# Expert weights in 8 KB pieces: one expert a load, gate before up before down, in a two-block fp32 kernel

## The chip, the cores and the metric

The kernel runs on one core of one Trainium2 chip. The metric is the device time of one execution in microseconds (us), lower is better. A timed run is one launch of the whole program; the profile is one further execution, recorded by the hardware profiler.

## The reference

Two transformer blocks follow one another on 512 tokens of 1024 channels, all in fp32. The first block mixes tokens in four ways (neighbourhood attention, gated delta net, differential attention, Fourier mixing) and ends in a mixture of experts; the second has latent attention, a gating unit, pooling and a dense feed-forward, twice. The change touches the mixture of experts alone:

```python
def expert_choice_ffn(h, w_router, w_gate, w_up, w_down):
    B, N, D = h.shape                      # 1, 512, 1024
    cap = EC_FACTOR * N // N_EXPERTS       # 64 tokens for each of 16 experts
    aff = jax.nn.softmax((h @ w_router).astype(F32), axis=-1)
    gate, idx = lax.top_k(jnp.swapaxes(aff, 1, 2), cap)
    xg = jax.vmap(lambda hb, ib: hb[ib])(h, idx)
    hid = jax.nn.silu(jnp.einsum('becd,edf->becf', xg, w_gate)) * jnp.einsum('becd,edf->becf', xg, w_up)
    y = jnp.einsum('becf,efd->becd', hid, w_down) * gate[..., None].astype(h.dtype)
    return jax.vmap(lambda yb, ib: jnp.zeros((N, D), yb.dtype).at[ib.reshape(-1)].add(yb.reshape(-1, D)))(y, idx)
```

Each expert has a gate and an up matrix of 1024 x 2048 and a down matrix of 2048 x 1024, 8 MB each, so the sixteen experts' weights are 384 units of 1 MB (402.7 million bytes), each read from HBM once.

## The kernel before

`block1` runs up to the router, `experts` does the mixture, `block2` the second block. `experts` takes the experts in eight pairs. In a pair the 64 tokens of expert A and the 64 of expert B stand side by side as 128 rows: `gather` (L1981) picks them with one-hot products into `xg`; the gate and up products (L2012) go to PSUM tiles `a`, rows 0 to 63 from one expert's weights and rows 64 to 127 from the other's; the hidden rows `hid` are SiLU of gate (ScalarE, L2020) times up (VectorE, L2021); four transposes (L2024) and a copy (L2026) make `hT`; the down products (L2033) gather in `y`; and eight products `o` with the one-hot matrix (L2048, L2049) add the result to the rows it came from (L2050). The pair is done in two halves `fp` of 1024 hidden columns each.

Weights come as *units* of 1 MB, 8 KB in each of 128 partitions. `expert_units` lists them in the order of use: a unit holds, for both experts of the pair, 1024 fp32 (4 KB) of one row per partition. `Stream` issues them all from SyncE's queue at L93, each into the next slot of a ring of slots that lie in several pools: 12 slots are there from the start of the output projection of block 1 (`ahead(12)`), 6 more come free there, and one, `w9`, with the pool of `experts`, 19 in all. A load waits only until its slot's earlier unit has been used. So SyncE's order is fixed by the list, and how far it runs ahead by the number of slots. `block2` then loads its own weights in the same queue (L283).

Of the kernel before, what the change touches and what calls it, by code (L numbers as in the profile page):

```python
# [6 lines left out]
F32 = mybir.dt.float32  # L7
# [33 lines left out]
class Ring:  # L41
    """slots of 8 KB per partition from several pools, taken in turn"""
# [10 lines left out]
class Carve:  # L53
    """arrays next to one another in tiles of 8 KB per partition"""
# [16 lines left out]
class Cut:  # L71
    """arrays next to one another in one tile"""
# [11 lines left out]
class Stream:  # L84
    """units of weights in the order of their use, loaded as far ahead as asked for"""
# [20 lines left out]
def prep2(tc, k, I, cs, ps, two):  # L106
    """everything of block 2 that does not depend on x"""
# [22 lines left out]
    # rope tables  # L130
# [18 lines left out]
def prep3(k, I, cs, ps, tmp):  # L149
    """the rest of it: rows over all partitions, and the matrices of the gating unit and of the pooling"""  # L150
# [34 lines left out]
def split(k, pool, src, shape, tag="", nb=4, eng=None):  # L185
    """(hi, lo) of an fp32 array, as tiles that the one-pass products take"""
    nc = k.nc
    n = shape[0] * shape[1]
    wsz = max(n, k.wsz)
    hi = pool.tile([P, wsz], F32R, tag="wh" + tag, name="wh", bufs=nb)  # L190
    lo = pool.tile([P, wsz], F32R, tag="wl" + tag, name="wl", bufs=nb)
    hv = hi[:, :n].rearrange("p (a b) -> p a b", a=shape[0])
    lv = lo[:, :n].rearrange("p (a b) -> p a b", a=shape[0])
    nc.scalar.activation(hv, src, AF.Copy)  # L194
    (eng or nc.vector).tensor_tensor(lv, src, hv.bitcast(F32), op=OP.subtract)  # L195
    return hv, lv
# [14 lines left out]
class Joint:  # L211
    """the final norm of the first block and the first norm of the second: x * g1 * g2 in two parts, and both sums of squares"""
# [24 lines left out]
    def done(self, ps, sp):  # L237
        """the factor of the final norm, and the inverse square and the factor of both"""
# [15 lines left out]
        # eps and the mean square after the final norm, times its inverse factor squared  # L254
# [15 lines left out]
def block2(tc, k, I, xT, out, ps):  # L270
# [3 lines left out]
    with ExitStack() as ctx:  # L274
# [20 lines left out]
        class Prep:  # L295
            """x * g in two parts, and the sum of squares of x over its channels"""
# [21 lines left out]
            def rstd(self):  # L318
                """mean square + eps, and its -1/2 power, [token, tile]"""
# [10 lines left out]
        def rowcast(pool, r):  # L330
            """[token, tile] -> the same row on all partitions"""
# [9 lines left out]
        def finish():  # L341
            """the final norm of the first block in its place"""
            rb = rowcast(sqp, pr.r0)
            for d in range(8):
                nc.vector.scalar_tensor_tensor(xT[:, d], xT[:, d], k.gf[:, d:d + 1], rb, op0=OP.mult, op1=OP.mult)

        def result(c):
            """half of the channels, token-major"""
# [12 lines left out]
        for l in range(2):  # L361
            win = I['w_in_2'][l].rearrange("(k p) f -> p k f", p=P)
            with tc.tile_pool(name=f"att{l}", bufs=1) as at:
                e1 = None
                # low-rank queries and keys/values, channel-major
# [37 lines left out]
                # token-major: shared rotary key, gates and values of the spatial unit, pool  # L403
                zn = at.tile([P, 4, 800], F32, name="zn")

                def rest(c):
                    """a part of these columns"""
# [19 lines left out]
                # queries, keys, values, token-major  # L427
# [23 lines left out]
                def queries(tb):  # L451
# [13 lines left out]
                    # sums of squares per head  # L465
# [6 lines left out]
                    # rotary part of the queries  # L472
# [12 lines left out]
                def keys(tb):  # L485
                    T2 = slice(2 * tb, 2 * tb + 2)
                    # keys
# [32 lines left out]
                def group(gi, c0, gn):  # L520
                    """the norm of a group of the mix, and its channels in two parts"""
# [17 lines left out]
                def gating():  # L539
                    # spatial gating unit  # L540
# [106 lines left out]
                def outs(h, mix, done, pt_):  # L647
                    """half of the rows of the out projection"""
# [33 lines left out]
                # out projection  # L682
# [3 lines left out]
            # feed-forward  # L686
# [55 lines left out]
def consts1():  # L742
# [40 lines left out]
    # first those that are needed beyond the first block's attention  # L783
# [19 lines left out]
def rev(ap, axis):  # L803
    """the same elements, one axis back to front"""
# [10 lines left out]
def exp_poly(nc, sp, out, x, n):  # L815
    """exp(x), x <= 0, to float32's accuracy"""
# [18 lines left out]
def block1(tc, k, I):  # L835
    """up to the router: x1 (channel-major), its norm token-major, slots and weights of the experts"""
# [16 lines left out]
    with ExitStack() as ctx:  # L853
# [29 lines left out]
        def wcols(c0, n, eng=None):  # L883
            """8 k-tiles of n columns of w_in, split"""
# [15 lines left out]
        def chan(w, c, z, src, n, ds=range(8)):  # L900
            """z[128 channels, n tokens]"""
# [4 lines left out]
        def modulation(cg, pool, unit):  # L906
            """2048 columns of the modulation; one step per unit of weights"""
# [17 lines left out]
        with tc.tile_pool(name="e1", bufs=1) as e1, tc.tile_pool(name="e2", bufs=2) as e2:  # L925
# [21 lines left out]
            # squares  # L947
# [9 lines left out]
            # shift and scale, of the rows and of the context's  # L957
# [5 lines left out]
            # shift and scale of two tiles of channels at a time, for both conditions, and these tiles of the normed rows  # L963
            def first(p):
                """the part of these tiles in the first convolution's channels"""
# [4 lines left out]
            for p in range(4):  # L970
# [6 lines left out]
                # the rows' tiles meanwhile  # L977
# [45 lines left out]
        p1c = ExitStack()  # L1023
        pc = p1c.enter_context(tc.tile_pool(name="pc", bufs=1))
        # places that stay free until the chain, for the weights of the other modulations
# [16 lines left out]
        def halves(out, z4, w, ctx):  # L1042
            """natural tiles -> pairs of an even chunk and the odd chunk that mirrors it"""
# [7 lines left out]
        # places of a convolution's rows that are free until the arrays of the other mixers come  # L1051
# [41 lines left out]
        def l2(kind, X, n, o, XT):  # L1093
            """divided by the norm of each head; channel-major too"""
# [27 lines left out]
        # gates  # L1122
# [38 lines left out]
        # by type of step: A runs the even chunk forward and the odd one backward, B the reverse  # L1161
# [34 lines left out]
        # products of keys within chunks  # L1196
# [23 lines left out]
        # decays  # L1220
# [26 lines left out]
        # the queries with the decay of their place, for both types of step  # L1247
# [35 lines left out]
        for t in range(2):  # L1283
            for q in range(4):
                rows = slice(32 * q, 32 * q + 32)
                fwd = q // 2 == t
                # the system is lower triangular: as it is forward, transposed backward
# [11 lines left out]
        # back: the inverse with its second index on the partitions, and for half of the blocks its first  # L1299
# [36 lines left out]
        cosv, sinv = (C(n).rearrange("p (t i) -> p t i", t=4) for n in ('cos', 'sin'))  # L1336

        def rope(x, n):
            """pairs of neighbours turned by the angles of their token, in place"""
# [27 lines left out]
        # the queries of each head, their first part twice, and their second part  # L1367
# [12 lines left out]
        def before(si):  # L1380
            """the inverse of the step's triangular systems, what it makes of the keys, and of the values"""
# [16 lines left out]
        def state(si, T, wn):  # L1398
            """the step's new values and the next state"""
# [51 lines left out]
        def dn_norm(ps_):  # L1451
            """norm and gate of two pairs of chunks"""
# [52 lines left out]
        for c in range(2):  # L1505
            z = zt("qz")
            chan(w, c, z, lat, 512)
            # each tile of queries back to front, as the bias comes
# [15 lines left out]
        def put(mx, j, z, s=None):  # L1524
            """channels of the mix in two parts"""
# [17 lines left out]
        # the keys of each head in both parts, the first one where the queries' second part is  # L1543
# [59 lines left out]
        def score(*qk):  # L1603
            """queries times keys"""
# [6 lines left out]
        def values(A, v, h, alt=False):  # L1611
            """weights times values [query, 64], by way of [key, query], three blocks of keys at a time"""
# [34 lines left out]

        def df_head(h):
# [41 lines left out]
            # by the root mean square of the head  # L1690
# [52 lines left out]
        # the out projection: the rows that are there before the last heads, then the others  # L1743
# [75 lines left out]
        def logits():  # L1819
            """of the channels up to 6 [token, expert], in the bank that the sums of squares come to as well"""  # L1820
# [62 lines left out]
        # the normed tokens, token-major  # L1883
# [6 lines left out]
        # the first pair's tokens by the number of those that come before each: larger, or as large and earlier  # L1890
# [40 lines left out]
def expert_units(I):  # L1931
    """the weights of a pair of experts after another, a megabyte at a time"""
    w = [I[n][0].rearrange("e (k p) f -> p e k f", p=P) for n in ('w_gate', 'w_up', 'w_down')]
    for e in range(0, 16, 2):
        for fp in range(2):
            for kk in range(8):
                for i in range(2):
                    yield w[i][:, e:e + 2, kk, fp * 1024:fp * 1024 + 1024], 2
            for kk in range(8 * fp, 8 * fp + 8):
                yield w[2][:, e:e + 2, kk], 2  # L1940


def experts(tc, k, I, prep, ps):
    """the tokens that each expert chose, through it, and added to the rows they came from"""
# [3 lines left out]
    def places(xp):  # L1948
        """of the other experts' tokens: the largest eight at a time, counted in the tokens' order"""
# [5 lines left out]
        nc.vector.tensor_copy(wk, z[0:16])  # L1955
        for i in range(8):
# [5 lines left out]
        nc.vector.tensor_tensor(wk, wk, cum, op=OP.mult)  # L1962
        z = ps.tile([P, 512], F32, tag="m", name="slot", bufs=2)
# [4 lines left out]
    with tc.tile_pool(name="x2", bufs=2) as xp:  # L1968
        k.stream.ring.order.append((xp, "w9", 1))
        for pr in range(8):  # L1970
# [16 lines left out]
            def slots():  # L1987
                """the slots in the order [slot, token], and the weight of the token in each"""
# [16 lines left out]
            for fp in range(2):  # L2005
# [131 lines left out]
```

## Time and profile before

| | |
|---|---|
| three timed runs | 2605.61, 2611.21, 2605.61 us (median 2605.61) |
| span of the profiled execution, first to last instruction | 2604.2 us |
| stage of the experts, from the first L2012 to the last L2049 | 579.4 to about 1540 us |
| TensorE's granted clock in that stage from 585 us on | 1.00 |
| rate of all DMAs, 620 to 1500 us | 408 GB/s |

The page gives no time of its own for the profiled execution beside the span; the median of the runs lies 1.4 us above the span, and that is taken for what lies around it. A view by stage gives, for a stretch, each engine's busy time and the rate of DMA; a view of DMA gives packets by size and the share of time that they took on the 16 DMA engines (over 100% where packets overlap); the timeline merges neighbouring instructions of one kind, and in brackets stands the idle time before the first and what ended it. The trace counts two MATMUL records for one fp32 product.

### The profile page before, as it was taken

The page shows a single profiled execution, that of the slowest core. Times are in us where ns is not written, and L with a number is a line of the kernel's source. Part 1 is how long each engine was busy: PE and PEld are TensorE (multiplying, and loading weights), DVE is VectorE, ACT ScalarE, POOL GpSimd, SP SyncE. Part 2 cuts the span into 40 slices and gives each one's busy share as a digit, 9 for nine tenths or more (in the row PEclk, how much of TensorE's full clock was granted, in tenths as well). Part 3 has the DMA queues.
Part 4 walks back from the last instruction along what each step waited for, and adds up shares of the span by engine and source line. Part 5 has one row for each costly group of instructions (what it writes and reads, how often), then busy time and mean ns, then how long its engine had stood idle before and what let it go on. Part 6 is the DMA issues. An engine that isn't in the chain of part 4 may idle for free. (4 is left out here: it accounts for less than half of the span.)

```text
span 2604.2 us, 31722 instructions
## 1 busy us (share of the span) xinstructions
PE 2420.6 (93%) x12919; PEld 1602.7 (62%) x12919; DVE 1040.3 (40%) x1839; ACT 700.7 (27%) x1362; POOL 254.3 (10%) x331
## 2 busy tenths in 40 slices
PE   6988999989999797989898889999999999999999
PEld 5768877763434242323233349778888897788887
DVE  5798347532111011010101036664444556644443
ACT  4522347520000000000000035432222354422221
POOL 1344445300000000000000012000000020000000
PEclk9998999989999999999999999999999999999999
DMA  8441100479999999999999972133332221322220
GB/s 270 149 145 47 48 22 17 150 258 399 407 408 408 409 408 408 409 409 409 409 409 409 409 254 86 49 113 97 98 97 87 65 82 49 113 97 89 91 96 33
DMA packets 214584, 547.75 MB, mean 210 GB/s; under 512 B 19183, under 2 KB 100903, under 8 KB 212263
## 3 DMA queue, kind: packets, MB, share of 16 engines
q1 hardware_dynamic: 208272, 544.39, 55.7%
q10 hardware_dynamic: 6167, 1.33, 0.3%
q8 instruction: 102, 1.67, 0.3%
q14 instruction: 43, 0.35, 0.0%
HBM read 543.56 MB, written 2.13 MB: 210 GB/s over the span
## 5 line engine op out<-in xcount | busy, mean ns | idle before, releaser
L2012 PE MATMUL a<-w,xg 128*64 128x512 f32 x2048 | 477.4, 598 | 59.7 <-DMA w<-in_w_up_dram 31.2
L2012 PEld LDWEIGHTS a<-w,xg 128*64 128x64 f32 x2048 | 139.3, 136 | 369.7 <-issue 236.6
L194 ACT ACTIVATE wh<-w 128x512 fp32r<-128x512 f32 (+3 forms) x304 | 202.6, 678 | 457.4 <-PE gu L201 226.6
L202 PE MATMUL gu<-hh,wl 128*128 128x512 f32 x704 | 278.1, 395 | 0.0
L2033 PE MATMUL y<-w,hT 128*64 128x512 f32 x1024 | 248.6, 599 | 31.1 <-DMA w<-in_w_down_dram 19.3
L201 PE MATMUL gu<-hl,wh 128*128 128x512 f32 x704 | 276.7, 393 | 0.0
L200 PE MATMUL gu<-hh,wh 128*128 128x512 f32 x704 | 273.8, 389 | 0.0
L195 DVE TENSOR_TENSOR wl<-w,wh 128x512 fp32r<-128x512 f32 (+3 forms) x304 | 223.8, 749 | 121.4 <-ACT wh L194 119.5
L2021 DVE TENSOR_TENSOR hid<-a,hid 128x512 f32<-128x512 f32 x32 | 22.1, 692 | 486.0 <-PE a L2012 486.0
L2033 PEld LDWEIGHTS y<-w,hT 128*64 128x64 f32 x1024 | 75.7, 136 | 182.0 <-issue 120.2
L2020 ACT ACTIVATE hid<-a 128x512 f32<-128x512 f32 x32 | 19.1, 597 | 550.8 <-PE a L2012 502.1
L201 PEld LDWEIGHTS gu<-hl,wh 128*128 128x128 f32 x704 | 132.4, 188 | 30.9
L200 PEld LDWEIGHTS gu<-hh,wh 128*128 128x128 f32 x704 | 132.5, 188 | 29.7
L202 PEld LDWEIGHTS gu<-hh,wl 128*128 128x128 f32 x704 | 132.8, 189 | 26.4
L200 PE MATMUL dn<-hid,wh 128*128 128x512 f32 x352 | 139.3, 401 | 0.0
L202 PE MATMUL dn<-hid,wl 128*128 128x512 f32 x352 | 137.7, 395 | 0.0
L201 PE MATMUL dn<-hid,wh 128*128 128x512 f32 x352 | 137.3, 394 | 0.0
L732 DVE TENSOR_TENSOR accT<-dn,accT 128x512 f32<-128x512 f32 x96 | 66.1, 691 | 125.7 <-PE dn L202 125.7
L241 POOL MEMSET gg<- 128x256 f32 x1 | 0.3, 314 | 960.3 <-PE y L2033 960.3
L1985 ACT ACTIVATE xg<-g,mT,sc 128x128 f32<-128x128 f32 x64 | 25.9, 454 | 208.2 <-PE g L1981 208.2
L1999 DVE COPY wt<-wt 64x1 f32<-64x1 f32 x16 | 2.5, 156 | 191.7 <-PE wt L1996 191.6
L201 PEld LDWEIGHTS dn<-hid,wh 128*128 128x128 f32 x352 | 66.1, 188 | 17.8 <-DVE hid L722 2.3
(695 smaller groups left out, 4057.5 us busy)
## 6 DMA issues: line engine op xcount, KB each, us to landing
w<-in_w_gate_dram SPq DMA_DIRECT2D x150, 1024.0 KB, 7.2
w<-in_w_up_dram SPq DMA_DIRECT2D x150, 1024.0 KB, 20.4
w<-in_w_down_dram SPq DMA_DIRECT2D x150, 1024.0 KB, 20.4
w<-in_w_mod_dram SPq DMA_DIRECT2D x24, 1024.0 KB, 9.7
w<-in_w_in_dram SPq DMA_DIRECT2D x16, 1024.0 KB, 5.3
w<-in_w_out_dram SPq DMA_DIRECT2D x8, 1024.0 KB, 4.9
wo<-in_w_out_dram SPq DMA_DIRECT2D x4, 1024.0 KB, 9.9
w<-in_w_in_dram SPq DMA_DIRECT2D x4, 576.0 KB, 3.8
```

Source lines behind the costliest of these rows:

```text
L194: nc.scalar.activation(hv, src, AF.Copy)
L195: (eng or nc.vector).tensor_tensor(lv, src, hv.bitcast(F32), op=OP.subtract)
L200: nc.tensor.matmul(out, a[0], b[0], start=start, stop=False)
L201: nc.tensor.matmul(out, a[0], b[1], start=False, stop=False)
L202: nc.tensor.matmul(out, a[1], b[0], start=False, stop=stop)
L732: nc.vector.tensor_tensor(xT[:, d], z, xT[:, d], op=OP.add)
L1985: nc.scalar.activation(xg[:, dd, :], g[:, d, :], AF.Identity, scale=k.sc2[:, dd:dd + 1], bias=k.mT[:, 0, 24 + dd:25 + dd])
L1999: nc.vector.tensor_copy(wt[64 * i:64 * i + 64], tp[64 * i:64 * i + 64, 0, i:i + 1])
L2012: nc.tensor.matmul(a[f][64 * i:64 * i + 64, :], xg[:, kk, 64 * i:64 * i + 64], u[:, i, f * 512:f * 512 + 512], start=kk == 0, stop=kk == 7)
L2020: nc.scalar.activation(hid, acc[0][f], AF.Silu)
L2021: nc.vector.tensor_tensor(hid, acc[1][f], hid, op=OP.mult)
L2033: nc.tensor.matmul(y[dh][64 * i:64 * i + 64, :], hT[j // 4][:, j % 4, 64 * i:64 * i + 64], u[:, i, dh * 512:dh * 512 + 512], start=fp == 0 ...
```

## The change

A unit now holds one expert alone: for gate and up one whole row of 2048 fp32 (8 KB) per partition, for down two neighbouring rows of 1024 (8 KB), for which partition p takes the rows 16p to 16p+15 of w_down instead of p, p+128, ... Units come for a pair as all of gate (16), all of up (16), all of down (16), the two experts in turn. The kernel follows: the halves `fp` are gone, four PSUM tiles gather gate for all 2048 columns, SiLU writes them to a `hid` of 16 x 128 columns in down's new row order, then the same four tiles gather up, and four groups of four transposes (`turn`) feed down. The work on the other experts' places (`places`) is cut into three steps. The scratch for dynamic DMAs is set to 1024 bytes, `hid` grows from 2 KB to 8 KB per partition, and the pool `ringB` has 9 slots instead of 8 (20 in all; 13 asked for at the start).

```diff
 def expert_units(I):
-    w = [I[n][0].rearrange("e (k p) f -> p e k f", p=P) for n in ('w_gate', 'w_up', 'w_down')]
+    w = [I[n][0].rearrange("e (k p) f -> p e k f", p=P) for n in ('w_gate', 'w_up')]
+    wd = I['w_down'][0].rearrange("e (p j) d -> p e j d", j=16)
     for e in range(0, 16, 2):
-        for fp in range(2):
+        for w_ in w:
             for kk in range(8):
                 for i in range(2):
-                    yield w[i][:, e:e + 2, kk, fp * 1024:fp * 1024 + 1024], 2
-            for kk in range(8 * fp, 8 * fp + 8):
-                yield w[2][:, e:e + 2, kk], 2
+                    yield w_[:, e + i, kk:kk + 1], 1
+        for j in range(0, 16, 2):
+            for i in range(2):
+                yield wd[:, e + i, j:j + 2], 2
...
-            for fp in range(2):
-                acc = [[ps.tile([P, 512], F32, tag="s", name="a", bufs=4) for f in range(2)] for w in range(2)]
+            hid = xp.tile([P, 16, P], F32, tag="hid", name="hid", bufs=1)
+            for w in range(2):
+                acc = [ps.tile([P, 512], F32, tag="s", name="a", bufs=4) for f in range(4)]
                 for kk in range(8):
-                    for a in acc:
-                        u = unit()
-                        for f in range(2):
+                    us = [unit() for i in range(2)]
+                    for f in range(4):
+                        for i in range(2):
+                            nc.tensor.matmul(acc[f][64 * i:64 * i + 64, :], xg[:, kk, 64 * i:64 * i + 64], us[i][:, 0, f * 512:f * 512 + 512], start=kk == 0, stop=kk == 7)
...
+                for f in range(4):
+                    h, a = hid[:, :, 32 * f:32 * f + 32], acc[f].rearrange("p (q j) -> p j q", j=16)
+                    if w == 0:
+                        nc.scalar.activation(h, a, AF.Silu)
+                    else:
+                        nc.vector.tensor_tensor(h, a, h, op=OP.mult)
...
+            turn(0)
+            for g in range(4):
+                if g < 3:
+                    turn(g + 1)
+                for jj in range(2):
+                    us = [unit() for i in range(2)]
+                    for r in range(2):
+                        j = 2 * jj + r
+                        for dh in range(2):
                             for i in range(2):
-                                nc.tensor.matmul(a[f][64 * i:64 * i + 64, :], xg[:, kk, 64 * i:64 * i + 64], u[:, i, f * 512:f * 512 + 512], start=kk == 0, stop=kk == 7)
+                                nc.tensor.matmul(y[dh][64 * i:64 * i + 64, :], hT[g][:, j, 64 * i:64 * i + 64],
+                                                 us[i][:, r, dh * 512:dh * 512 + 512], start=g + j == 0, stop=g + j == 6)
...
-            rb = k.rbx.enter_context(tc.tile_pool(name="ringB", bufs=8))
-            k.stream = Stream(nc, Ring((ring, "w", 2), (rb, "w", 8), (k.lt, "lt", 2), (k.b8, "b8", 6)), expert_units(I))
-            k.stream.ahead(12)
+            rb = k.rbx.enter_context(tc.tile_pool(name="ringB", bufs=9))
+            k.stream = Stream(nc, Ring((ring, "w", 2), (rb, "w", 9), (k.lt, "lt", 2), (k.b8, "b8", 6)), expert_units(I))
+            k.stream.ahead(13)
...
-    nc = _bacc.Bacc("TRN2", target_bir_lowering=False, num_devices=1)
+    nc = _bacc.Bacc("TRN2", target_bir_lowering=False, num_devices=1, dynamic_dma_scratch_size=1024)
```

On SyncE's queue, where the expert stream begins behind the last loads of block 1's output weights (`wo`), the kernel before issues:

```order
L1753 DMA wo<-in_w_out_dram 128x8x256 x3
L93 DMA w<-in_w_gate_dram 128x2x1024
L93 DMA w<-in_w_up_dram 128x2x1024
...
L93 DMA w<-in_w_down_dram 128x2x1024 x8
L93 DMA w<-in_w_gate_dram 128x2x1024
L93 DMA w<-in_w_up_dram 128x2x1024
```

and the changed one:

```order
L1753 DMA wo<-in_w_out_dram 128x8x256 x3
L93 DMA w<-in_w_gate_dram 128x2048 x16
L93 DMA w<-in_w_up_dram 128x2048 x16
L93 DMA w<-in_w_down_dram 128x2048 x16
L93 DMA w<-in_w_gate_dram 128x2048 x16
```

Each load is still 128 x 8 KB, but in one run per partition instead of two (for down too, since its two rows lie behind one another), and the order within a pair is by matrix.

On TensorE, in the last pair, from the small product `wt` (L1996) to the first `o`, stand before (here a product counts once):

```order
L1996 MATMUL wt<-aff,oh 128x2 x4
L2012 MATMUL a<-w,xg 64x512 x31
L2024 MATMUL tp<-c_64,hid 128x128 x4
L2033 MATMUL y<-w,hT 64x512
L2024 MATMUL tp<-c_64,hid 128x128 x4
L2033 MATMUL y<-w,hT 64x512 x31
L2012 MATMUL a<-w,xg 64x512 x64
L2024 MATMUL tp<-c_64,hid 128x128 x4
L2033 MATMUL y<-w,hT 64x512
L2024 MATMUL tp<-c_64,hid 128x128 x4
L2033 MATMUL y<-w,hT 64x512 x31
L2048 MATMUL o<-oht,ysb 128x512 x2
```

and now, from the same product (L2001 in the changed file):

```order
L2001 MATMUL wt<-aff,oh 128x2 x4
L2018 MATMUL a<-w,xg 64x512 x95
L2039 MATMUL tp<-c_64,hid 128x128 x8
L2053 MATMUL y<-w,hT 64x512 x2
L2039 MATMUL tp<-c_64,hid 128x128
L2053 MATMUL y<-w,hT 64x512 x6
L2039 MATMUL tp<-c_64,hid 128x128 x7
L2053 MATMUL y<-w,hT 64x512 x56
L2069 MATMUL o<-oht,ysb 128x512 x2
```

The number of products of each kind is the same; the two passages from up to down in a pair have become one, in front of which all four columns' tiles must be multiplied, and behind it the remaining transposes stand among the down products.

## Rows read from the trace of the kernel before

**Rows 1.** The page: the span, TensorE and DMA in 40 slices.
```profile
span 2604.2 us, 31722 instructions
PE   6988999989999797989898889999999999999999
DMA  8441100479999999999999972133332221322220
GB/s 270 149 145 47 48 22 17 150 258 399 407 408 408 409 408 408 409 409 409 409 409 409 409 254 86 49 113 97 98 97 87 65 82 49 113 97 89 91 96 33
```

**Rows 2.** View by stage: engines' busy us, granted clock, DMA share, GB/s.
```profile
585.00:650.00 65.00, 64.37 (x318) 24.79 (x316) 18.19 (x36) 4.58 (x8) 0.00 (x0) 1.00 1.02 398
910.00:1040.00 130.00, 113.49 (x513) 41.04 (x510) 16.39 (x26) 8.86 (x17) 0.00 (x0) 1.00 1.03 408
1900.00:2100.00 200.00, 199.15 (x896) 163.17 (x895) 95.22 (x145) 64.20 (x101) 4.99 (x4) 1.00 0.23 71
```

**Rows 3.** Waits of TensorE, 450 to 1600 us: total, times, longest.
```profile
PE a L2012 <- DMA w<-in_w_up_dram: 31.2, 49, 1.3
PE a L2012 <- DMA w<-in_w_gate_dram: 28.4, 47, 0.7
PE y L2033 <- DMA w<-in_w_down_dram: 19.3, 32, 0.7
```

**Rows 4.** Timeline of TensorE, one pair: start, length, what, [idle before].
```profile
1036.87 0.73 PE L2048 MATMUL o<-oht,ysb 128*128 128x512 f32 x2
...
1043.91 3.84 PE L1981 MATMUL g<-oh,xn 128*128 128x128 f32 x32 [0.19 <-DVE accT L2050]
1047.68 7.09 PE L2012 MATMUL a<-w,xg 128*64 128x512 f32 x32
1054.70 2.05 PE L1981 MATMUL g<-oh,xn 128*128 128x128 f32 x16
...
1103.26 1.94 PE L2012 MATMUL a<-w,xg 128*64 128x512 f32 x8 [0.62 <-DMA w<-in_w_up_dram]
...
1138.99 1.94 PE L2012 MATMUL a<-w,xg 128*64 128x512 f32 x8 [0.61 <-DMA w<-in_w_up_dram]
1140.93 0.66 PE L2024 MATMUL tp<-c,hid 128*128 128x128 f32 x4
1142.37 1.07 PE L2033 MATMUL y<-w,hT 128*64 128x512 f32 x2 [0.78 <-DVE hT L2026]
```

**Rows 5.** View of DMA, 620 to 1500 us: expert units, 4 KB runs.
```profile
DMA packets 93134, 359.45 MB, mean 408 GB/s; under 512 B 5478, under 2 KB 5478, under 8 KB 93096
...
q1 hardware_dynamic: 93096, 358.91, 102.3%
```

**Rows 6.** View of DMA, 11 to 36 us: w_mod and w_in, 1 KB runs.
```profile
DMA packets 8356, 8.79 MB, mean 352 GB/s; under 512 B 141, under 2 KB 8236, under 8 KB 8355
...
q1 hardware_dynamic: 8355, 8.78, 108.5%
```

**Rows 7.** View of DMA, 41 to 44 us: w_mod, 8 KB runs.
```profile
DMA packets 181, 1.28 MB, mean 427 GB/s; under 512 B 20, under 2 KB 20, under 8 KB 29
...
q1 hardware_dynamic: 181, 1.28, 102.7%
```

**Rows 8.** View of DMA, 78.6 to 80.6 us, in 40 slices: one w_in unit, 1 KB.
```profile
GB/s 266 164 532 348 164 184 246 225 348 369 348 348 389 348 451 369 348 389 369 369 430 348 389 410 348 410 389 369 410 369 389 410 348 389 430 348 410 369 389 410
```

**Rows 9.** Waits of SyncE's queue, 555 to 592 us.
```profile
SPq L93 <- DVE slot L1929: 16.8, 1, 16.8
SPq L93 <- PE a L2012: 14.6, 5, 7.4
```

**Rows 10.** View of DMA, 505 to 582 us, in 40 slices of 1.9 us.
```profile
GB/s 72 171 367 9 136 338 307 315 368 309 381 423 409 394 306 311 415 417 115 0 0 0 230 340 385 400 340 313 349 302 353 419 264 126 0 0 217 319 17 0
```

**Rows 11.** Timeline of TensorE where the stage begins and ends.
```profile
579.39 7.09 PE L2012 MATMUL a<-w,xg 128*64 128x512 f32 x32
...
1529.27 1.94 PE L2033 MATMUL y<-w,hT 128*64 128x512 f32 x8 [0.66 <-DMA w<-in_w_down_dram]
1531.19 0.73 PE L2048 MATMUL o<-oht,ysb 128*128 128x512 f32 x2
```

**Rows 12.** Groups by line, page: count, busy us, mean ns, idle before.
```profile
L2021 DVE TENSOR_TENSOR hid<-a,hid 128x512 f32<-128x512 f32 x32 | 22.1, 692 | 486.0 <-PE a L2012 486.0
L2020 ACT ACTIVATE hid<-a 128x512 f32<-128x512 f32 x32 | 19.1, 597 | 550.8 <-PE a L2012 502.1
```

More of the change, by code (lines that the diff above doesn't have):

```diff
@@ L1955, in places @@
         nc.vector.tensor_copy(wk, z[0:16])
+        yield
         for i in range(8):
@@ L1962, in places @@
         nc.vector.tensor_tensor(wk, wk, cum, op=OP.mult)
+        yield
         z = ps.tile([P, 512], F32, tag="m", name="slot", bufs=2)
@@ L2004, in experts @@
             y = [ps.tile([P, 512], F32, tag="z", name="y", bufs=2) for i in range(2)]
-            for fp in range(2):
-                acc = [[ps.tile([P, 512], F32, tag="s", name="a", bufs=4) for f in range(2)] for w in range(2)]
+            hid = xp.tile([P, 16, P], F32, tag="hid", name="hid", bufs=1)
+            for w in range(2):
+                acc = [ps.tile([P, 512], F32, tag="s", name="a", bufs=4) for f in range(4)]
                 for kk in range(8):
-                    for a in acc:
-                        u = unit()
-                        for f in range(2):
-                            for i in range(2):
-                                nc.tensor.matmul(a[f][64 * i:64 * i + 64, :], xg[:, kk, 64 * i:64 * i + 64], u[:, i, f * 512:f * 512 + 512], start=kk == 0, stop=kk == 7)
-                    if fp == 0 and kk in (1, 3):
-                        gather(kk // 2 + 2)
-                    if fp == 0 and kk == 3:
-                        oht, wt = slots()
-                hT = []
-                for f in range(2):
-                    hid = xp.tile([P, 512], F32, tag="hid", name="hid", bufs=1)
-                    nc.scalar.activation(hid, acc[0][f], AF.Silu)
-                    nc.vector.tensor_tensor(hid, acc[1][f], hid, op=OP.mult)
-                    tp = ps.tile([P, 4, P], F32, tag="m", name="tp", bufs=2)
-                    for j in range(4):
-                        nc.tensor.transpose(tp[:, j, :], hid[:, j * P:(j + 1) * P], k.ident)
-                    hT.append(xp.tile([P, 4, P], F32, tag="hT", name="hT", bufs=2))
-                    nc.vector.tensor_copy(hT[f], tp)
-                if pr == 0 and fp == 0:
-                    places(xp)
-                for j in range(8):
-                    u = unit()
-                    for dh in range(2):
-                        for i in range(2):
-                            nc.tensor.matmul(y[dh][64 * i:64 * i + 64, :], hT[j // 4][:, j % 4, 64 * i:64 * i + 64],
-                                             u[:, i, dh * 512:dh * 512 + 512], start=fp == 0 and j == 0, stop=fp == 1 and j == 7)
@@ new lines, in experts @@
+                    us = [unit() for i in range(2)]
+                    for f in range(4):
+                        for i in range(2):
+                            nc.tensor.matmul(acc[f][64 * i:64 * i + 64, :], xg[:, kk, 64 * i:64 * i + 64], us[i][:, 0, f * 512:f * 512 + 512], start=kk == 0, stop=kk == 7)
+                    if w == 0 and kk in (1, 3):
+                        gather(kk // 2 + 2)
+                    if w == 0 and kk == 3:
+                        oht, wt = slots()
+                    if pr == 0 and w == 0 and kk == 5:
+                        others = places(xp)
+                        next(others)
@@ new lines, in experts, with turn @@
+                if pr == 0:
+                    next(others, None)
+                for f in range(4):
[4 more added lines that the diff above has]
+                        nc.vector.tensor_tensor(h, a, h, op=OP.mult)
+            hT = {}
+            def turn(g):
+                tp = ps.tile([P, 4, P], F32, tag="m", name="tp", bufs=2)
+                for j in range(4):
+                    nc.tensor.transpose(tp[:, j, :], hid[:, 4 * g + j], k.ident)
+                hT[g] = xp.tile([P, 4, P], F32, tag="hT", name="hT", bufs=2)
+                nc.vector.tensor_copy(hT[g], tp)
@@ L2037, in experts @@
             ysb = xp.tile([P, 1024], F32R, tag="xg", name="ysb")
-            yl = [xp.tile([P, 512], F32R, tag=t_, name="yl", bufs=b_) for t_, b_ in (("hid", 1), ("hT", 2))]
+            yl2 = xp.tile([P, 2048], F32R, tag="hid", name="yl", bufs=1)
+            yl = [yl2[:, 512 * i:512 * i + 512] for i in range(2)]
             for i in range(2):
```

## The prediction

> **What bounds the kernel now.** I read the page first, for its slices [rows 1]: from slice 9 to slice 22, some 910 of 2604 us, the DMA row stands at 9 and the rate at 399 to 409 GB/s and does not move, while TensorE's row stands between 7 and 9. Everywhere else DMA is mostly idle and TensorE full. The view by stage says the same in numbers [rows 2]: between 910 and 1040 us TensorE is busy 113.49 of 130 us with DMA at a share of 1.02, while between 1900 and 2100 us it is busy 199.15 of 200. So two limits: DMA in the expert stage, TensorE after it. The waits of TensorE tell whether its idle time is DMA's [rows 3]: 128 waits, 31.2 + 28.4 + 19.3 = 78.9 us, all on expert units, none longer than 1.3 us. The timeline of one pair shows the shape [rows 4]. After the `o` products and `gather`, TensorE takes units that have already landed at 7.02 us for four (1047.68 to 1054.70), 1.76 us a unit; later it has caught up and each unit costs a wait of 0.6 us, from 1103.26 to 1138.99 fourteen units in 35.73 us, 2.55 a unit. That is DMA's pace, not TensorE's.
>
> How far is TensorE from being the bound? A pair needs 48 units x 1.76 = 84.2 us, `gather` 3.84 + 2 x 2.05 = 7.9, the `o` part 1036.87 to 1043.91 = 7.0, two passages from up to down of 1.44 each = 2.9 (1140.93 to 1142.37): about 102 us, beside which a few small products stand. DMA takes 48 x 2.57 = 123 (below). The distance is some 20 us a pair.
>
> **The runs.** This is the main term: the same bytes in runs of 8 KB instead of 4 KB. Before, 358.91 MB pass in 880 us, so 1,048,576 bytes take 2.571 us [rows 5]. That the runs are 4 KB follows from the counts: 93096 - 5478 = 87618 packets for 358.91 MB are 4096 bytes each, and the 5478 short ones are 16 per load. What a run costs beyond its bytes I take from other loads of this kernel, since one unit is 1 MB in each:
> - 1 KB runs, `w_mod` and `w_in` from 11 to 36 us: 8.78 MB in 25 us, 2.986 us for a unit [rows 6]. An engine has 64 runs there, and 16 in an expert unit, so 48 runs more cost 0.415 us, 8.6 ns each. Eight runs fewer, as in the change, save 0.069 us: 2.502 us.
> - 8 KB runs, `w_mod` from 41 to 44 us: 1.28 MB in 3 us, 427 GB/s, 2.457 us for a unit [rows 7]. 181 - 29 = 152 of its packets are 8 KB or more, so a run of 8 KB stays in one piece. The stretch is short, but it is the operation itself.
> - The other bound: in the last 24 slices of a single `w_in` unit, also 1 KB runs, the mean is 385 GB/s, 2.724 us [rows 8]. By that a run costs only (2.724 - 2.571) / 48 = 3.2 ns, and eight fewer save 0.026: 2.546 us.
>
> I take 2.49: between the first two, nearer the one with the long stretches. The saving is 0.081 us a unit.
>
> The Trainium skill has a rule on this step ("DMA: Bandwidth & Descriptors", Why small descriptors are slow): a packet costs about three cycles beside one per 32 bytes. By it 4 KB are 131 cycles and 8 KB 259, a unit would take 2.571 x 259/262 = 2.542 us, and the time would be 2596 us. The 1 KB rows above ask for nearly three times that cost, the single unit about as much as the rule.
>
> **How many units.** Not all 384 pay it. The queue of SyncE first waits for places of block 1; its last such wait, 16.8 us, is for `slot` L1929 [rows 9], and DMA stands still several times before 582 us [rows 10]. By then the ring is full, 19 units. From there on a load waits only for TensorE to use a slot, which it does faster than DMA fills them, and the stream does not pause again until its last unit, which TensorE waits for until 1529.27 us [rows 11]. So 365 units at 2.571 = 938.4 us lie between; the 582 to 1529 that the rows show is some 8 us more, the start and the trailing end of the stream, which I leave as it is.
>
> After: 20 slots. The thirteenth of the first units needs no place of block 1 and DMA had idle time there [rows 10], so 20 units are there and 364 remain: 364 x 2.49 = 906.4 us. Against 938.4 that is -32.0.
>
> **What is added.** Units are used in twos, because the products of the two experts alternate. The first slot is used again after two units instead of one, 1.76 us later; and behind the last landing TensorE has nearly two units left instead of one, again +1.76. Together +3.5. SyncE issues as many loads of the same size in the same order of slots, 384 modulo 19 and modulo 20 both being 4, so block 2's first loads find their slots after the same units as before.
>
> The passage from up to down: only when the last of four multiplications (0.69 us each, L2021 [rows 12]) is done can the first four transposes (0.66) go, then a copy and its hand-over (0.78): 2.2 us once a pair instead of 1.44 twice. Should reading PSUM with a step of 16 elements double the multiplication and SiLU (0.60), four multiplications in a row are 5.5 us and the passage below 8. DMA's lead of 15 to 20 us a pair hides either; in the last pair 32 us of down units follow in which TensorE gains 0.73 a unit. Without that cover it would be up to 5 us a pair. The longest time in which TensorE uses no unit is 1036.87 to 1047.68, 10.8 us or 4.3 units; of 20 slots enough stay in flight. `places` moves on VectorE under the up products of the first pair and costs nothing for the same reason. The smaller scratch concerns no load of this kernel, which issues its DMAs from SyncE and ScalarE.
>
> Sum: -32.0 + 3.5 = -28.5. Made against the span, 2604.2 to 2575.7; with the 1.4 us that the median of the runs has more, **2577 us**.
>
> **The rivals.**
> *A run costs little.* With 2.546 us a unit [rows 8]: 364 x 2.546 = 926.7, -11.7 + 3.5 = -8.2, 2597 us. For it: the middle of that unit. Against it: 427 GB/s with 8 KB runs [rows 7]. Chance 0.18, a quarter of it within 0.3%.
> *The stride of down* (the other side). Partition p now reads at 64 KB x p; before, neighbouring partitions lay 4 KB apart. The rows show that where runs lie can matter: `w_mod`, whose rows are 24 KB long, takes 2.986 us [rows 6], `w_in`, whose rows are 11 KB, 2.724 [rows 8], 0.262 more for runs of the same size. If down's 128 units lose that against today, +33.5 us; gate and up save 236 x 0.081 = 19.1, with the slot and the twos 18.2 in all: 2605.6 + 15.3 = 2621 us. It decides from a loss of 18.2 / 128 = 0.142 us, that is 2.713 us or 386 GB/s for down. Against it: gate and up units with 8 KB between partitions run no slower than down with 4 KB (one flat rate through all [rows 5]). Chance 0.12, two thirds of it slower. The same page of the Trainium skill (Latency and other measured facts) lists losses at row pitches that are large powers of two, 3% at 512 KiB and a quarter at 2 MiB; 64 KiB it does not list, and no run here shows one.
> *No gain*: something other than the run, HBM or the ports, sets 408 GB/s. Then -2.6 + 3.5, 2606 to 2607 us. Rows 7 speak against it. Chance 0.05.
> *TensorE or the slots become the bound* because of the twos and the single passage: from a cost of 15 us a pair on, which nothing above reaches; at 20 us a pair it would be about 2645 us. Chance 0.03.
>
> **How the numbers follow.** The forecast has 0.62; its own bounds are 2565 (2.457 us a unit: 894.3, -40.6) and 2581 (2.502: 910.7, -24.2). A measurement of this kernel tells about 0.3%, 8 us, from no change. Faster: 0.62 + 0.13 + 0.02 = 0.77; within: 0.05 + 0.05 + 0.02 = 0.12; slower: 0.08 + 0.03 = 0.11. The range runs from the lower bound of the run's cost, 2564, to just above the first rival, 2599; outside lie down's stride, no gain and TensorE as the bound.
>
> **What would show it.** In the middle of the stage 8 KB packets, half as many, at some 421 GB/s; a pair 119.5 us instead of 123; TensorE waiting about 1.5 us before every two units (2 x 2.49 - 3.51); the last down product near 1500 us; block 2 as long as before. Wrong would be a rate that differs between gate and down (the stride), waits of SyncE with DMA below its rate (slots), or a stage without waits on DMA (TensorE).

## The result, and the profile after

The changed kernel takes 2574.32 us in the median (2571.08 to 2577.10, four runs) against 2605.61 (2605.37 to 2611.21, four runs on the same chip): a ratio of 0.9873, 95% interval 0.9858 to 0.9887. The forecast was 2577, between 2564 and 2599. Timed again beside experiments 5 and 6 it took 2574.99 us against 2600.51, 0.9898 (0.9883 to 0.9912). So the gain is 31.3 us in the one set of runs and 25.5 in the other.

The page of the changed kernel, in the lines that answer to [rows 1]:

```profile
span 2575.3 us, 31691 instructions
PE   7988999989999999999999999999999999999999
DMA  8441200378999999999999952232222221333220
GB/s 268 153 149 34 63 22 18 118 294 366 421 421 421 421 421 421 421 421 421 421 421 421 421 195 83 65 129 86 97 90 80 66 83 50 115 98 98 91 90 33
```

The flat part stands at 421 GB/s where 407 to 409 stood. TensorE's row is now at 9 through the same slices, which looks as if TensorE had become the bound; the sixth experiment below says that it has not. The view by stage, in the stretches of [rows 2] (busy us of TensorE, its weight loads, VectorE, ScalarE and GpSimd, then granted clock, DMA share, GB/s):

```profile
585.00:650.00 65.00, 64.10 (x320) 24.82 (x318) 19.46 (x38) 5.78 (x10) 0.00 (x0) 1.00 0.98 403
910.00:1040.00 130.00, 125.42 (x556) 53.50 (x556) 14.58 (x23) 8.89 (x19) 0.00 (x0) 1.00 1.01 421
1900.00:2100.00 200.00, 199.12 (x989) 168.08 (x987) 101.11 (x175) 75.96 (x132) 13.05 (x7) 1.00 0.28 87
```

The view of DMA between 600 and 1480 us answers to [rows 5]:

```profile
DMA packets 50857, 370.58 MB, mean 421 GB/s; under 512 B 5653, under 2 KB 5653, under 8 KB 5653
...
q1 hardware_dynamic: 50817, 370.01, 101.1%
```

Between the short packets (16 per load) and 8 KB there is none: 50817 - 5653 = 45164 packets of 8192 bytes make 369.98 of the 370.01 MB. A unit takes 1.0486 MB / (370.01 MB / 880 us) = 2.494 us; the forecast had 2.49.

Where the 28.9 us between the two spans lie is read from the timeline of TensorE, first the changed kernel's stage at both ends (answers to [rows 11]):

```profile
582.73 7.09 PE L2018 MATMUL a<-w,xg 128*64 128x512 f32 x32
...
1499.20 3.65 PE L2053 MATMUL y<-w,hT 128*64 128x512 f32 x12 [0.57 <-DMA w<-in_w_down_dram]
1502.82 0.73 PE L2069 MATMUL o<-oht,ysb 128*128 128x512 f32 x2
```

From the first expert product to the first `o` of the last pair the stage took 951.8 us before (579.39 to 1531.19) and takes 920.1 now, 31.7 less. The time up to the stage is 3.3 longer (582.7 against 579.4), the time behind it 0.5 shorter (1072.5 against 1073.0). The 3.3 us belong to block 1, whose arithmetic the change does not touch; the last section comes back to them. The length of the stage, in contrast, repeats well: 920.1 and 920.3 us in the two profiles of the changed kernel.

The waits of TensorE from 450 to 1600 us, those on DMA and on the passage (answers to [rows 3]):

```profile
PE y L2053 <- DMA w<-in_w_down_dram: 9.6, 18, 0.6
PE tp L2039 <- DVE hid L2033: 7.0, 8, 1.2
PE y L2053 <- DVE hT L2041: 2.8, 8, 0.4
```

Of the 78.9 us of waits on gate, up and down units 9.6 are left, all on down. This is not because TensorE waits less for DMA. At the end of one pair and in the next, which begins near 1023 us:

```profile
1009.17 4.47 PE L2053 MATMUL y<-w,hT 128*64 128x512 f32 x16 [0.55 <-DMA w<-in_w_down_dram]
1014.15 4.40 PE L2053 MATMUL y<-w,hT 128*64 128x512 f32 x16 [0.50 <-DMA w<-in_w_down_dram]
...
1033.54 7.09 PE L2018 MATMUL a<-w,xg 128*64 128x512 f32 x32
1040.56 2.05 PE L1986 MATMUL g<-oh,xn 128*128 128x128 f32 x16
...
1053.96 49.76 PE L2018 MATMUL a<-w,xg 128*64 128x512 f32 x190
1104.95 1.09 PE L2039 MATMUL tp<-c,hid 128*128 128x128 f32 x8 [1.23 <-DVE hid L2033]
1106.38 1.93 PE L2053 MATMUL y<-w,hT 128*64 128x512 f32 x4 [0.35 <-DVE hT L2041]
```

Sixteen records (two units) take 3.5 us when the weights are there (32 in 7.02, from 1033.54 to 1040.56) and 4.4 when they are not, and they come every 4.98 us, two units of DMA. Part of the wait stands inside the group: of the sixteen records from 1009.17 on, ten begin by 1011.37 and the other six from 1011.75 on, about one unit of DMA after the first. Products of the two experts alternate, so some can go while the other expert's unit is missing, and the profile counts the stretched group as busy.

### The profile page after: what moved, and what is told of

It reads as the page before. It is cut to its first block, busy times and chain, and to the rows that moved or that the text cites. A ratio compares the mean times of both kernels' runs of the same rounds, so it can differ in the third digit from the quotient of the medians.

```text
span 2575.3 us, 31691 instructions
## 1 busy us (share of the span) xinstructions
PE 2464.7 (96%) x12919; PEld 1662.6 (65%) x12919; DVE 1040.0 (40%) x1839; ACT 699.1 (27%) x1362; POOL 257.6 (10%) x331
## 5 line engine op out<-in xcount | busy, mean ns | idle before, releaser
L2018 PE MATMUL a<-w,xg 128*64 128x512 f32 x2048 | 498.0, 597 | 0.0
L2018 PEld LDWEIGHTS a<-w,xg 128*64 128x64 f32 x2048 | 178.9, 136 | 293.6 <-issue 282.8
L2053 PE MATMUL y<-w,hT 128*64 128x512 f32 x1024 | 266.6, 599 | 12.7 <-DMA w<-in_w_down_dram 9.6
L2053 PEld LDWEIGHTS y<-w,hT 128*64 128x64 f32 x1024 | 91.3, 136 | 170.2 <-issue 131.0
L2062 ACT ACTIVATE ysb<-y,wt 128x512 fp32r<-128x512 f32 x16 | 11.0, 688 | 505.7 <-PE y L2053 504.8
```

Source lines behind the costliest of these rows:

```text
L2018: nc.tensor.matmul(acc[f][64 * i:64 * i + 64, :], xg[:, kk, 64 * i:64 * i + 64], us[i][:, 0, f * 512:f * 512 + 512], start=kk == 0, stop=k ...
L2053: nc.tensor.matmul(y[dh][64 * i:64 * i + 64, :], hT[g][:, j, 64 * i:64 * i + 64], us[i][:, r, dh * 512:dh * 512 + 512], start=g + j == 0, ...
L2062: nc.scalar.activation(yh, y[i], AF.Copy, scale=wt)
```

## The experiments

In all but the last the changed kernel is the base. Two numbers are given for each: the ratio to the kernel before, run on the same chip, and the length of the stage in the profile, read as above.

**1. All units in 4 KB runs, everything else as changed.**

```diff
-            for kk in range(8):
-                for i in range(2):
-                    yield w_[:, e + i, kk:kk + 1], 1
+            for kk in range(0, 8, 2):
+                for c in range(2):
+                    for i in range(2):
+                        yield w_[:, e + i, kk:kk + 2, 1024 * c:1024 * c + 1024], 2
...
-                yield wd[:, e + i, j:j + 2], 2
+                yield wd[:, e + i, j // 2:j // 2 + 9:8], 2
```

The products follow the new order of rows, the same in number. Expected: 

> The changed kernel with every unit cut into two runs of 4 KB again (two rows by half the columns; for down two rows that do not lie behind one another); order by matrix, one expert a unit, 20 slots stay. If the length of the run is the cause: the rate falls from 421 back to 408 GB/s, 364 units x (2.571 - 2.494) = +28 us on the changed kernel's 2574.3, about 2602 us, ratio to before 0.998 to 1.000. If order, slots or the single passage gave the gain: 421 GB/s need not fall, about 2574 us, ratio 0.988.

Measured: 2606.47 us, ratio 1.0000 (0.9987 to 1.0012); stage 949.3 us. The view of DMA, 640 to 1440 us:

```profile
DMA packets 84799, 327.27 MB, mean 409 GB/s; under 512 B 4987, under 2 KB 4987, under 8 KB 84766
...
q1 hardware_dynamic: 84766, 326.79, 102.3%
```

The gain is gone with the long runs: the order by matrix, the twos, the single passage, the smaller scratch and the slot together are worth 951.8 - 949.3 = 2.5 us of the stage. Against the changed kernel the stage is 29.2 us longer, 0.080 us for each of 364 units.

**2. Down alone in 4 KB runs** (the second half of the diff above). Expected: 

> The changed kernel with 4 KB runs for down alone (64 KB from partition to partition stays). If only the run counts: 128 units x 0.077 = +9.9 us, 2584 us, ratio 0.992, and down units at 2.57 us beside gate and up at 2.49. If the stride of down cost something that the long run hid, more than 10 us; if down gained nothing from its long run, 2574 us.

Measured: 2579.59 us, ratio 0.9904 (0.9889 to 0.9919); stage 929.4 us, 9.3 more than the changed kernel (9.9 expected). The view of DMA from 640 to 760 us, in 40 slices of 3 us, shows both rates in one pair, down at 407 to 411 at either end and gate and up at about 421 between:

```profile
GB/s 408 408 414 422 412 426 421 423 423 421 421 423 421 415 423 421 423 421 423 423 418 418 421 418 426 423 415 426 426 408 408 407 408 408 411 411 408 410 410 411
```

So down has its third of the gain from its own runs.

**3. Down's rows taken so that a unit is one piece of 1 MB.**

```diff
-    wd = I['w_down'][0].rearrange("e (p j) d -> p e j d", j=16)
+    wd = I['w_down'][0].rearrange("e (k p r) d -> p e k r d", p=P, r=2)
...
-                yield wd[:, e + i, j:j + 2], 2
+                yield wd[:, e + i, j // 2], 2
...
-                    h, a = hid[:, :, 32 * f:32 * f + 32], acc[f].rearrange("p (q j) -> p j q", j=16)
+                    h = hid[:, 4 * f:4 * f + 4].rearrange("p (k r) q -> p k r q", k=2)
+                    a = acc[f].rearrange("p (k q r) -> p k r q", k=2, r=2)
```

Expected: 

> The changed kernel with down's rows taken as 256 k + 2 p + r, so a unit is one piece of 1 MB and neighbouring partitions lie 8 KB apart instead of 64 KB; runs of 8 KB stay, and a group of four transposes now needs one of the four column tiles only. If the stride of down costs nothing: within 3 us of 2574, ratio 0.986 to 0.989, 421 GB/s. If it costs something: down units faster than 2.49 us, and the time below 2571 us.

Measured: 2572.21 us, ratio 0.9876 (0.9858 to 0.9894), 421 GB/s, stage 920.1 us, as long as with 64 KB between partitions. The stride costs nothing here, and that the first transposes need one column tile instead of four saves nothing either. The version is as good as the changed kernel, not better.

**4. One slot less.**

```diff
-            rb = k.rbx.enter_context(tc.tile_pool(name="ringB", bufs=9))
+            rb = k.rbx.enter_context(tc.tile_pool(name="ringB", bufs=8))
...
-            k.stream.ahead(13)
+            k.stream.ahead(12)
```

The count of `ringB` in the ring is 8 as well. Expected: 

> The changed kernel with 19 slots and 12 units asked for at the start, as before. If the slot is worth one unit loaded ahead: +2.5 us, about 2577 us, ratio 0.989. If slots limit the stream: the rate falls below 421 GB/s and the time rises by more than 5 us. If the slot does nothing: 2574 us.

Measured: 2575.76 us, ratio 0.9884 (0.9868 to 0.9900), which does not tell 2.5 us from nothing. The stage does: 922.7 us, 2.6 more, at the same 421 GB/s. The slot is worth one unit that is loaded ahead, and it does not carry the rate.

**5. Gate and up in 2 KB runs.**

```diff
-            for kk in range(8):
-                for i in range(2):
-                    yield w_[:, e + i, kk:kk + 1], 1
+            for kk in range(0, 8, 4):
+                for c in range(4):
+                    for i in range(2):
+                        yield w_[:, e + i, kk:kk + 4, 512 * c:512 * c + 512], 4
```

Expected: 

> The changed kernel with gate and up in runs of 2 KB (four rows by a quarter of the columns). If each run costs the same 9.6 ns that lie between 2.571 and 2.494 us (8 runs an engine): 24 runs more, +0.231 us, 2.725 us a unit or 385 GB/s, 236 such units, +54 us, about 2629 us, slower than before by 0.9%. If a run costs only 3.2 ns as the prediction's rival had it: +0.077, +18 us, about 2592 us.

Measured: 2627.49 us, ratio 1.0100 (1.0085 to 1.0115); stage 972.7 us, 52.6 more than the changed kernel (54 expected). In the middle of gate and up units, 665 to 675 us, 385 GB/s had been expected:

```profile
DMA packets 1945, 3.86 MB, mean 386 GB/s; under 512 B 61, under 2 KB 61, under 8 KB 1944
```

**6. Half of the down products left out.** Only the first of the two rows that a unit holds per partition is multiplied; all weights are loaded.

```diff
-                    for r in range(2):
+                    for r in range(1):
...
-                                                 us[i][:, r, dh * 512:dh * 512 + 512], start=g + j == 0, stop=g + j == 6)
+                                                 us[i][:, r, dh * 512:dh * 512 + 512], start=g + j == 0, stop=g + j == 5)
```

Expected: 

> The changed kernel with half of the down products left out (every second row of hidden; all weights are still loaded), which takes about 8 x 1.76 = 14 us of TensorE's work out of each pair. If DMA alone sets the stage: 421 GB/s as before, and only the tail is shorter, 2 to 3 us, about 2572 us. If TensorE has its share in the pace: up to 14 us a pair, 2460 us or more, down to that.

Measured: 2575.71 us, ratio 0.9896 (0.9879 to 0.9912), beside 0.9898 for the changed kernel in the same set of runs; stage 918.6 us. The groups by line, first on the page of the changed kernel, then on that of this run:

```profile
L2018 PE MATMUL a<-w,xg 128*64 128x512 f32 x2048 | 498.0, 597 | 0.0
L2053 PE MATMUL y<-w,hT 128*64 128x512 f32 x1024 | 266.6, 599 | 12.7 <-DMA w<-in_w_down_dram 9.6
```

```profile
L2018 PE MATMUL a<-w,xg 128*64 128x512 f32 x2048 | 515.1, 597 | 0.2 <-DMA w<-in_w_up_dram 0.2
...
L2053 PE MATMUL y<-w,hT 128*64 128x512 f32 x512 | 216.2, 603 | 44.4 <-DMA w<-in_w_down_dram 41.6 <-DVE hT L2041 2.8
```

512 records of 1024 are gone, at 0.22 us each (32 in 7.02 us) over 110 us of work, and what TensorE no longer does turns up as waits (44.4 us where 12.7 stood) and as longer groups (515.1 us of gate and up where 498.0 stood, 0.42 us for each down record where 0.26 stood). The stage is 1.5 to 1.7 us shorter than in the two profiles of the changed kernel, which is its tail: 1.90 us from the last wait on down to the first `o`, where 3.62 stood. So TensorE, busy 125.42 of 130 us in the changed kernel, still does not set the pace.

**The changed kernel again**, beside 5 and 6. Expected: 

> The changed kernel once more, unchanged, as the mark for the others on the same chip: 2571 to 2577 us, ratio 0.986 to 0.989.

Measured: 2574.99 us, ratio 0.9898 (0.9883 to 0.9912), stage 920.3 us.

**7. The loads alone**, in a kernel of its own: 24 loads of 2 MB for each length of run, one after the other.

```diff
+        for kb, u0 in ((4, 0), (8, 16), (16, 32), (1, 0), (2, 16), (4, 32), (8, 0)):
+            f = 256 * kb
+            w = flat.rearrange("(u n p f) -> u p n f", p=P, f=f, n=16 // kb)
+            for u in range(24):
+                v = sl.tile([P, 4096], F32, tag="w", name="w", bufs=10)
+                nc.sync.dma_start(v.rearrange("p (n f) -> p n f", f=f), w[u0 + u])
```

Expected: 

> Loads alone: none of the computation is done and the output is filled with zeros. Seven stretches of 24 loads of 2 MB (16 KB per partition, ten slots) from w_gate, in runs of 4, 8, 16, 1, 2, 4 and 8 KB. If a run costs 9.6 ns beside its bytes wherever it is loaded, 2.417 + n x 0.0096 us per MB with n runs an engine: 1 KB 3.03 us or 346 GB/s, 2 KB 385, 4 KB 408, 8 KB 420, 16 KB 2.456 us or 427. If the loss per run comes from TensorE and the others using the memory at the same time, all stretches are faster and closer together. If there is a ceiling near 421 GB/s, 16 KB gives no more than 8 KB.

The view of DMA of that kernel, whole span in 40 slices of 22 us; the stretches follow one another as 4, 8, 16, 1, 2, 4 and 8 KB:

```profile
GB/s 360 410 410 410 409 415 421 423 421 422 422 429 430 431 427 426 374 348 348 348 348 348 353 387 387 387 387 387 393 410 410 409 410 410 419 422 422 422 422 376
```

The queue's own row in the stretches 400 to 480 us (1 KB), 520 to 620 (2 KB), 640 to 740 (4 KB), 760 to 860 (8 KB) and 260 to 340 (16 KB), packets, MB, share:

```profile
q1 hardware_dynamic: 27408, 27.85, 110.1%
q1 hardware_dynamic: 19173, 38.68, 105.1%
q1 hardware_dynamic: 10319, 40.96, 102.6%
q1 hardware_dynamic: 5484, 42.21, 101.3%
q1 hardware_dynamic: 2347, 34.23, 100.5%
```

For 1,048,576 bytes that is 3.012, 2.711, 2.560, 2.484 and 2.450 us. From one to the next 32, 16, 8 and 4 runs an engine fall away, so a run costs 9.4, 9.4, 9.5 and 8.4 ns. This is counted per engine; whether the 16 engines lose it or what feeds them, no run tells apart. With no engine computing, 4 KB and 8 KB run at 410 and 422 GB/s, as they do beside a busy TensorE (409 and 421): the loss is the run's, not the neighbours'. And 421 is no ceiling, since 16 KB reaches 428.

## Why the prediction was right, step by step

*DMA bounds the stage.* Right; experiment 6 shows it for the changed kernel: 110 us less work on TensorE changed nothing but the tail. Only the first pair, which finds its first units already loaded, goes at TensorE's pace: its first `o` comes 94.0 us after the first product at 421, 409 and 386 GB/s alike (the changed kernel, experiments 1 and 5) and 82.0 us after it with half of the down products left out. The later pairs take that up. From the second pair to the last, the first `o` of a pair follows that of the pair before it after 119.3 us on average, where 123.8 stood (forecast 119.5 instead of 123).

*The runs: 0.081 us a unit on 364 units.* Right: 2.571 to 2.494 us a unit is 0.077, and experiment 1 gives 29.2 us / 364 = 0.080, of which 0.073 are the flat rate's (2.567 to 2.494) and the rest lies at the ends of the stream. Of the three sources the two that were weighed together, [rows 6] and [rows 7], were the good ones: the measured 2.494 lies between their 2.502 and 2.457, near the first, and a run costs 9.4 ns where [rows 6] had given 8.6.

*The first rival, a run costs little.* Wrong, with its source: the middle of a single unit [rows 8] had given 3.2 ns. Experiment 5 gives 9.3 ns (52.6 us on 236 units with 24 runs more each), experiment 7 8.4 to 9.5. The Trainium skill's rule of about three cycles a packet ("DMA: Bandwidth & Descriptors", Why small descriptors are slow) led the prediction to an estimate near the rival's, 2.542 us a unit or 3.7 ns a run. The runs do not bear the rule out: they show about two and a half times as much, 3% for the step from 4 to 8 KB where the estimate has 1.1%. The prediction's "nearly three times", from the 8.6 ns of [rows 6], is 2.3 times by the same estimate.

*The stride of down, the rival on the other side.* Excluded by experiments 2 and 3: with 8 KB runs 421 GB/s at 64 KB and at 8 KB between partitions, with 4 KB runs 407 to 411 at 64 KB, as before at 4 KB. The rows that the rival rested on do not show an effect of the place either: 1 KB runs from one flat piece go at 348 GB/s (experiment 7), hardly other than those of [rows 6], nearly all from `w_mod` with its rows of 24 KB, at 352.

*The slot, one unit less to load under TensorE's eyes.* Right: 2.6 us (experiment 4), forecast 2.57.

*The twos, +3.5 us.* Both parts are there as forecast. The tail from the last wait on down to the first `o` grew from 1.92 us (1529.27 to 1531.19) to 3.62. And the first slot is free later: in the 10 us that begin with the stage's first product, in slices of 0.25 us, DMA starts in the 12th slice before, but in the 19th in the changed kernel and in experiment 1, about 1.75 us later:

```profile
GB/s 0 0 0 0 0 0 0 0 0 0 0 16 115 82 213 180 360 328 377 377 442 426 393 442 361 213 295 262 279 377 393 410 360 328 377 377 344 279 311 442
GB/s 0 0 0 0 0 0 0 0 0 0 0 0 0 0 0 0 0 0 229 295 0 33 229 426 459 524 328 393 426 459 492 393 393 426 393 492 426 426 360 459
GB/s 0 0 0 0 0 0 0 0 0 0 0 0 0 0 0 0 0 0 33 131 115 197 131 295 246 344 328 295 393 377 393 410 328 426 344 410 360 229 344 279
```

*What the sum left as it is.* This term was mis-sized: the some 8 us for the start and the trailing end of the stream, which the prediction took as unchanged. From the first product to the end of the last wait on down 949.9 us passed before, 916.5 now and 945.7 in experiment 1. The units that had to come in that time take 365 x 2.571 = 938.4, 364 x 2.494 = 907.8 and 364 x 2.567 = 934.4 us at the flat rate. So 11.5, 8.7 and 11.3 us are left, where the later start should have turned the 11.5 into 13.2. In the first 60 us SyncE's queue moved 22.27, 23.09 and 21.82 MB, which is 5.4, 5.1 and 6.6 us behind the flat rate; after 930, 900 and 930 us (377.11, 376.29 and 377.17 MB) the three are still as far behind, so the rest, 6.1, 3.6 and 4.7 us, falls to the last 16 to 20 us before that wait. Why the ends of the stream cost less now was not tried and stays open. The 2.5 us that experiment 1 gains in the stage come out of the same terms: -2.6 for the slot, +3.5 for the twos, -1.4 for a unit of 2.567 instead of 2.571 us and -1.9 at the ends.

*The passage from up to down costs nothing.* Not tested alone, but nothing speaks against it: experiment 1 has the single passage too, and its stage is no longer than before. The passage takes 2.7 us, from 1103.72 to 1106.38 (forecast 2.2), with a wait of 1.23 us before the transposes and one of 0.35 before the first down product. VectorE's multiplication did not grow with the step of 16 elements, 691 ns where [rows 12] had 692:

```profile
L2033 DVE TENSOR_TENSOR hid<-a,hid 128x512 f32<-128x512 f32 x32 | 21.9, 691 | 331.5 <-PE a L2018 331.1
```

*What would show it.* The rate (421), the packets, the end of the last down products (1502.8, forecast near 1500) and block 2 came as forecast. TensorE's waits of 1.5 us before every two units did not: they are 0.5 before down and none before gate and up, because part of the products start without the second unit. The prediction had named a stage without waits on DMA as the sign of TensorE as the bound; whoever had looked for the waits alone would have read just that.

*The sum.* The forecast for the stage is -32.0 + 3.5 = -28.5. Measured are -30.6 at the flat rate (938.4 to 907.8), +3.5 for the twos (1.75 and 1.70) and about -4.6 at the ends of the stream, which the forecast had left at nothing: -31.7. On the profiled execution block 1 took 3.3 us back, so the span came out at 28.9 less. That this is so close to the forecast is partly luck: the mechanism and its main term are right, but two amounts that the forecast did not have, -4.6 at the ends of the stream and +3.3 in block 1, nearly cancel.

## What to carry to other kernels

Where DMA's rate is flat over a stage, take the time of a unit and count the runs per engine in it; two loads of other run lengths in the same trace give the cost of a run, if they are read from stretches in which the queue is full (the lone unit of [rows 8] gave a third of it). Lengthening the runs is then worth that cost times the runs saved, times the units that lie on the path. Of a stage whose bound is a flat rate, a busy TensorE says little: take work out of it and see whether the time moves. Compare stages by their own length: it repeated to 0.2 us in the two profiles here, where whole runs of the same kernel differed by 6.

## What the runs showed that was not expected

Without computation a run's cost is the same from 1 to 8 KB, 9.4 to 9.5 ns on an engine, and 8.4 from 8 to 16 KB. Beside TensorE's work the lengths of the stage give 9.1 to 10.0 ns between 2 and 8 KB (experiments 1, 2 and 5); other lengths were not tried there. From experiment 7 an estimate for runs of 16 KB in this kernel is 364 x (2.484 - 2.450) = 12 us more; it needs slots of 16 KB and another order of gate's and up's rows, and was not tried.

A single `w_in` unit moves its 1 KB runs at 385 GB/s in its middle [rows 8], a queue full of 1 KB runs at 348 in experiment 7, from one flat piece of memory. Why the lone unit is faster was not tried.

Block 1, in which the change touches no arithmetic, reached the first expert product between 573.0 us (experiment 2) and 584.9 (experiment 1). The granted clock between 520 and 570 us was 0.87 and 0.83 in these two, 0.90 in the profile of before and 0.88 in that of the changed kernel, so this stretch does not order the four by itself. The mean granted clock of the whole execution does: 0.989 (573.0 us), 0.988 before (579.4), 0.985 in the changed kernel (582.7) and 0.984 (584.9), while it stood at 1.00 through the stage of the experts. What lowers it in block 1 was not tried; two profiles of the same changed kernel differ by 2.1 us there (582.7 and 580.6). The whole spread is wider than every term of the sum but the first.
